# Strassen's seven parts for the inner quarter of two of FFN's products, not one

## The chip, the cores and the metric

The kernel runs on one core of one Trainium2 chip. The metric is the device time of one execution in microseconds: the median of three runs before the change is 1860.95 us (1859.37 to 1862.06).

## The reference, cut to what matters

Two layers, each with a half-step SwiGLU, a gated mixer and a second half-step SwiGLU, on 512 tokens of width 1024; the hidden width of SwiGLU is 2816. The change touches SwiGLU alone, which runs four times (the four FFNs).

```python
def swiglu(x, w_in, w_out):
    gu = x @ w_in
    g, u = jnp.split(gu, 2, axis=-1)
    return (jax.nn.silu(g) * u) @ w_out

for l in range(DEPTH):
    x = x + 0.5 * swiglu(rms_norm(x, ffn1_norm[l]), ffn1_w_in[l], ffn1_w_out[l])
    x = x + mixer(rms_norm(x, mix_norm[l]), ...)
    x = x + 0.5 * swiglu(rms_norm(x, ffn2_norm[l]), ffn2_w_in[l], ffn2_w_out[l])
```

## The kernel before, in words

**Precision.** Every operand of a product is split into a high part (fp32r, by ScalarE's copy) and a low part (operand less high part, by VectorE), and a product is three matmuls: high by high, high by low, low by high. For weights these are `Item.upper` and `Item.lower`: `whi` (L199, L201) and `wlo` (L206, L208).

**Weights.** They lie in DRAM as granules of 128 x 1024 (0.5 MB). `stage_items` writes the list of items in the order in which the products use them; `Stream` loads eight items ahead (`FETCH`) into nine buffers named `raw`, from SyncE's queue (L158). Where a granule is needed as a sum, a second transfer adds another granule to the loaded one, on GpSimd's queue (L160), or VectorE adds one buffer to another (`Item.sum`, L194). `whi` and `wlo` have three buffers each, so splitting runs at most some two granules ahead of TensorE.

**FFN's first product.** The 2816 columns of gate and up are 256 plain ones (`cl`) and five blocks of 512 each. A block's product (512 tokens by 1024, times 1024 by 512 gate and 512 up) is a two-by-two product of halves, which Strassen's scheme makes of seven products, numbered 1 to 7: the weights' quarters are a, b (gate) and c, d (up), and the operands of x are `acts[1]` to `acts[7]`. One product is two granules, 24 matmuls of 128x512 into two PSUM banks (`product`, L386 to L389). `snap` (L620) copies a bank to SBUF, `less` (L625) subtracts a copy from a bank, `gate` (L755) applies silu, and `times` (L761) multiplies gate by up. The result is transposed by TensorE into `at` tiles (`to_at`, L643, L647), the second product's operands.

**Pairs.** Blocks 1 and 2, and 3 and 4, form pairs. In both blocks of a pair product 2 multiplies the same lower-left quarter of x, by b of the first block and by b of the second. Side by side these make a two-by-two product again, which is done in seven inner parts of 6 matmuls each (`inner`, `inner_parts`, `inner_split`) instead of 2 x 24. Five inner parts stand in the first block and two in the second (`INNER`), and each is joined to the block's sums by a VectorE instruction of 128x512 (L833, L846, L847, L854, L857, L863, L870 in `pair_block`).

**FFN's second product.** `steps` lists its seven products in three chunks of columns (`o`, L386 to L389). Its operand 4 is a difference of two `at` tiles, made by VectorE (`comb`, L774), in the last FFN by ScalarE's negation and an adding transfer from SBUF to SBUF on GpSimd's queue (L1135, L1136).

**Order.** Each engine's instructions run in the order of its own queue. In the first block of the first FFN, and at the ends of the second products, the order is written out by hand; elsewhere a scheduler has set it. TensorE starts with nine matmuls on zeros (`WARM`, L146) while the first loads come.

Of the kernel before, what the change touches and what calls it, by code (L numbers as in the profile page):

```python
# [17 lines left out]
P = 128  # L18
# [11 lines left out]
WARM = 9  # L30
# [5 lines left out]
ORDER_P = (1, 5, 6, 7, 3, 4)  # L36
INNER = (((5, 1), (6, 5), (7, 2), (3, 6), (4, 3)), ((6, 7), (7, 4)))
# [61 lines left out]
def encoder_kernel(  # L99
# [120 lines left out]
    def stage_items():  # L220
        items, st = [], 0

        def add(*a, **k):
            items.append(Item(*a, stage=st, **k))
# [40 lines left out]
        def ffn(s):  # L265
            first = not items
            for g in range(4):
                add(Raw((s, "cl", g)), parts=2 if first and g < 2 else 1, pieces=2 if first and g == 0 else 1)
            for j in range(NB):
                if not j:  # L270
                    four(s, lambda q: q, j, (1024, 1024), ORDER_0 if first else ORDER_W)
                    continue
                if j in PAIRS:
                    key = [[(s, "b", j + z, g) for g in range(2)] for z in range(2)]
                    a, b, c = Raw(key[0][0]), Raw(key[0][1]), Raw(key[1][0], 1024, key[0][0])
                    d, d2 = Raw(key[1][1], 1024, key[1][0]), Raw(key[1][1])
                    parts = {1: (a, None, True), 2: (b,), 3: (d, b), 4: (d2,), 5: (d,), 6: (d, a), 7: (c,)}
                inner = dict(INNER[j not in PAIRS])
                for m in strassen(s, lambda q: q, j, (1024, 1024), ORDER_P):
                    if m in inner:  # L280
                        add(*parts[inner[m]])
                add(*parts[inner[0]]) if 0 in inner else None
# [344 lines left out]
    def stage_ffn(norm, nxt, late):  # L627
# [57 lines left out]
        def inner_parts(src):  # L685
# [7 lines left out]
            fine["t"] = t  # L693

        def inner_split():
            t = fine.pop("t")
            h = slot(F32R, "vh", (4, 2, P))
            l = scope_pool[0].tile([P, 4, 2, P], F32R, tag="vl", name=nm("vl"), bufs=1)
            split(h, l, t)
            fine.update({5: (h[:, 0], l[:, 0]), 6: (h[:, 1], l[:, 1]), 7: (h[:, 2], l[:, 2]), 4: (h[:, 3], l[:, 3])})  # L700
            for m, (i, b) in ((1, (0, 0)), (2, (1, 0)), (3, (1, 1))):
                fine[m] = [z[1][:, 2 * i : 2 * i + 2, b * P : (b + 1) * P] for z in (hx, lx)]
# [10 lines left out]
        with tc.manual_schedule(engines={mybir.EngineType.DVE, mybir.EngineType.Activation}) if first else nullcontext():  # L713
# [11 lines left out]
            inner_parts(b21)  # L725
# [95 lines left out]
        kept = {}  # L821

        def pair_block(jb, late_at):

            one = jb in PAIRS
# [4 lines left out]
            if one:  # L830
                qa = kept["a"] = bank("qA")
                inner(qa, 1, True)
                V.tensor_tensor(s1[:, 0, :], qa, s1[:, 0, :], ALU.add)  # L833
# [3 lines left out]
            qa = kept["a"]  # L837
            if one:
                qb = bank("qB")
                inner(qb, 5, True)  # L840
                tb = kept["s"] = slot(F32, "sq", (2, T))[:, 0, :]
                S.activation(tb, qb, AF.Copy)
            else:
                tb = kept["s"]
                inner(qa, 7, False)
                V.tensor_tensor(tb, qa, tb, ALU.subtract)  # L846
                V.tensor_tensor(s1[:, 1, :], tb, s1[:, 1, :], ALU.subtract)  # L847
# [3 lines left out]
            if one:  # L851
                qc = bank("qC")
                inner(qc, 2, True)
                V.tensor_tensor(s1[:, 0, :], qc, s1[:, 0, :], ALU.subtract)  # L854
            else:
                inner(qa, 4, False)
                V.tensor_tensor(s1[:, 0, :], qa, s1[:, 0, :], ALU.subtract)  # L857
                z1 = gate(s1, 0)
            product(pa, acts[7], K4, False, again=True)
            less(pa, sb)  # L860
            if one:
                inner(qa, 6, False)
                V.tensor_tensor(s1[:, 1, :], qa, s1[:, 1, :], ALU.add)  # L863
# [3 lines left out]
            times(z2, [sb[:, 0, :], sb[:, 1, :]], 1)  # L867
            if one:
                inner(qb, 3, False)
                V.tensor_tensor(s1[:, 1, :], qb, s1[:, 1, :], ALU.subtract)  # L870
                z1 = gate(s1, 0)
            if jb == NB - 1:
# [4 lines left out]
            late_at += [(z2, 1, 2 + 4 * jb, 4), (z1, 0, 2 + 4 * jb, 4)]  # L877
# [222 lines left out]
        for i, (m, c, _) in enumerate(steps):  # L1100
# [32 lines left out]
            if late and m == 6:  # L1133
# [1011 lines left out]
```

## Time and profile before

| what | value |
|---|---|
| median of three runs | 1860.95 us |
| profiled execution | 1859.66 us |
| its span on the core | 1857.9 us |
| TensorE, VectorE, ScalarE, GpSimd busy | 99%, 84%, 65%, 11% |
| matmuls and transposes | 9561 |
| read from HBM | 404.49 MB |

A row of a group names line, engine, operation, out<-in and count, then busy time, mean of one in ns, idle time before it, and what ended that. A row of a window names the stretch, its length, each engine's busy time with the number of instructions, the granted clock (1.00 is full), the share of the 16 transfer engines and GB/s. A busy PE is a union of overlapping matmuls: one shows 389 ns, while the next starts after some 227.

### The profile page before, as it was taken

The numbers are of one execution on the slowest core, as the hardware profiler recorded it, in microseconds if no ns is written. First come the engines' busy times: TensorE is split into PE (matmuls) and PEld (weight loads), VectorE is DVE, ScalarE is ACT, GpSimd is POOL, SyncE is SP. The second block draws the span as 40 slices with busy tenths as digits, with TensorE's granted clock in tenths as the row PEclk, the third lists the DMA queues.
The fourth block names the chain that finished last, engine by engine and source line by source line (L and its number), as shares of the span: only waits on it lengthen the run. The fifth ranks groups of instructions, "written<-read, shape, count | busy, mean of one in ns | idle before, by whom it ended". The sixth has DMA issues, their size and how long they took to land.

```text
span 1857.9 us, 26118 instructions
## 1 busy us (share of the span) xinstructions
PE 1847.8 (99%) x9561; PEld 1574.3 (85%) x9561; DVE 1556.5 (84%) x1915; ACT 1203.1 (65%) x1787; POOL 196.8 (11%) x235
## 2 busy tenths in 40 slices
PE   9999999999999999999999999999999999999998
PEld 7888888889998888888888888888899988888886
DVE  8888899758879787889978788996687797878999
ACT  6766666758656656666665666667676576656665
POOL 0010010100211011101001110110002100110010
PEclk9999999999999999999999999999999999999999
DMA  9788788875998479869757986987649985798695
GB/s 299 228 248 222 226 237 265 255 190 137 247 258 218 133 209 258 231 200 266 238 147 208 254 231 201 258 270 239 199 131 262 234 227 131 221 243 238 197 274 182
DMA packets 118384, 413.94 MB, mean 223 GB/s; under 512 B 13408, under 2 KB 13536, under 8 KB 118256
## 3 DMA queue, kind: packets, MB, share of 16 engines
q1 hardware_dynamic: 85712, 297.78, 45.7%
q0 software_dynamic: 32112, 113.71, 32.6%
q8 instruction: 75, 1.23, 0.3%
q10 hardware_dynamic: 432, 0.79, 0.1%
q14 instruction: 53, 0.43, 0.1%
HBM read 404.49 MB, written 6.29 MB: 221 GB/s over the span
## 4 chain that ended last, share of the span: by engine, by line
PE 97%; DMA 1%; DVE 1%; issue 0%; ACT 0%; POOL 0%; ACTq 0%; DVEq 0%; SPq 0%; POOLq 0%
PE A L386 9%; PE A L389 9%; PE A L387 9%; PE o L389 7%; PE o L386 7%; PE o L387 7%; PE B L386 5%; PE B L387 5%; PE B L389 5%; PE ps L386 3%; PE ps L387 3%; PE ps L389 3%; PE tr L643 2%; PE cl L387 2%; PE cl L389 2%; PE cl L386 2%
## 5 line engine op out<-in xcount | busy, mean ns | idle before, releaser
L208 DVE TENSOR_TENSOR wlo<-raw,whi 128x1024 fp32r<-128x1024 f32 (+1 forms) x540 | 638.7, 1191 | 170.3 <-ACT whi L201 169.3
L201 ACT ACTIVATE whi<-raw 128x1024 fp32r<-128x1024 f32 (+1 forms) x540 | 555.2, 1034 | 317.8 <-PE A L387 89.7
L160 POOL DMA_DIRECT2D raw<-in_wst_dram x186 | 161.4, 873 | 1458.9 <-DMA raw<-in_wst_dram 766.5
L194 DVE TENSOR_TENSOR raw<-raw,raw 128x1024 f32<-128x1024 f32 (+1 forms) x144 | 171.2, 1193 | 2.7
L387 PE MATMUL A<-whi,xl 128*128 128x512 f32 x320 | 124.5, 389 | 0.0
L386 PE MATMUL A<-whi,xh 128*128 128x512 f32 x320 | 124.5, 389 | 0.0
L199 ACT ACTIVATE whi<-raw 128x1024 fp32r<-128x1024 f32 x84 | 87.1, 1037 | 42.1 <-issue 21.5
L206 DVE SCALAR_TENSOR_TENSOR wlo<-raw,whi 128x1024 fp32r<-128x1024 f32 x84 | 99.8, 1196 | 4.6 <-ACT whi L199 4.5
L389 PE MATMUL A<-wlo,xh 128*128 128x512 f32 x320 | 92.1, 389 | 0.0
L620 ACT ACTIVATE sn<-A 128x512 f32<-128x512 f32 x96 | 56.2, 591 | 46.4 <-PE A L389 46.4
L755 ACT ACTIVATE th<-sn,r 128x512 f32<-128x512 f32 x80 | 56.1, 715 | 46.2 <-DVE sn L625 42.5
L389 PEld LDWEIGHTS A<-wlo,xh 128*128 128x128 f32 x320 | 60.1, 188 | 12.5
L387 PEld LDWEIGHTS A<-whi,xl 128*128 128x128 f32 x320 | 60.1, 188 | 12.5
L386 PEld LDWEIGHTS A<-whi,xh 128*128 128x128 f32 x320 | 60.1, 188 | 12.4
L386 PE MATMUL B<-whi,t1h 128*128 128x512 f32 x160 | 63.0, 394 | 0.0
L386 PE MATMUL A<-whi,t2h 128*128 128x512 f32 x160 | 62.5, 391 | 0.0
L387 PE MATMUL B<-whi,xl 128*128 128x512 f32 x160 | 62.3, 390 | 0.0
L387 PE MATMUL B<-whi,t1l 128*128 128x512 f32 x160 | 62.3, 389 | 0.0
L387 PE MATMUL A<-whi,t2l 128*128 128x512 f32 x160 | 62.3, 389 | 0.0
L386 PE MATMUL A<-whi,t3h 128*128 128x512 f32 x160 | 62.2, 389 | 0.0
L387 PE MATMUL A<-whi,t3l 128*128 128x512 f32 x160 | 62.2, 389 | 0.0
L386 PE MATMUL B<-whi,xh 128*128 128x512 f32 x160 | 62.2, 389 | 0.0
(498 smaller groups left out, 4909.2 us busy)
## 6 DMA issues: line engine op xcount, KB each, us to landing
raw<-in_wst_dram SPq DMA_DIRECT2D x503, 512.0 KB
raw<-in_wst_dram POOLq DMA_DIRECT2D x200, 512.0 KB, 8.2
raw<-in_wst_dram SPq DMA_DIRECT2D x28, 256.0 KB
vc<-vd SPq DMA_DIRECT2D x28, 256.0 KB
bm<-in_near_dram SPq DMA_DIRECT2D x16, 384.0 KB
vd<-v SPq DMA_DIRECT2D x8, 512.0 KB
dft<-in_dft_dram POOLq DMA_DIRECT2D x4, 514.0 KB, 8.3
x<-in_xin_dram SPq DMA_DIRECT2D x4, 512.0 KB
```

Source lines behind the costliest of these rows:

```text
L160: z = G.dma_start(out=self.t, in_=wst[GRAN_AT[plus]][:, 0 : self.n], accum_op=ALU.add)
L194: V.tensor_tensor(self.raw.t, self.raw.t, self.add.t, ALU.add)
L199: S.activation(self.out[0][:, cs], self.raw.t[:, cs], AF.Copy, scale=-1.0)
L201: S.activation(self.out[0][:, cs], self.raw.t[:, cs], AF.Copy)
L206: self.last = V.scalar_tensor_tensor(lo, t, -1.0, hi.bitcast(F32), ALU.mult, ALU.subtract)
L208: self.last = V.tensor_tensor(lo, t, hi.bitcast(F32), ALU.subtract)
L386: PE.matmul(ps, lh, rh, start=start, stop=False, skip_group_check=again)
L387: PE.matmul(ps, *((lh, rl) if w == "l" else (ll, rh)), start=False, stop=False, skip_group_check=again)
L389: PE.matmul(ps, *((ll, rh) if w == "l" else (lh, rl)), start=False, stop=stop, skip_group_check=again)
L620: S.activation(t[:, b, :], ps[b], AF.Copy)
L643: PE.transpose(tr[:, k, b * P : (b + 1) * P], a[:, b, (q + k) * P : (q + k + 1) * P], ident)
L755: S.activation(th[:, b, :], g[:, b, :], AF.Silu, scale=norm.r[:, c : c + 1])
```

## The change

1. In a pair, product 4 of both blocks multiplies the same quarter of x as well (`t4`, from `b21 - b22`), by d of the first block and by d of the second. Both products 4 are taken out, and seven more inner parts d1 to d7 come in, with operands of their own (`inner_parts("d", b21)`, two splits). `pair_block`, called for each block, becomes `pair_blocks`, called for each pair. Part d2 is accumulated into the bank of the first block's upper half, and d4 into that of the second block's, so that fewer joins are needed. The first block now has six inner parts, the second eight.
2. Operand 4 of the second product is made by ScalarE and an adding transfer in all four FFNs.
3. `WARM` is 12 instead of 9.

```diff
-WARM = 9
+WARM = 12
-ORDER_P = (1, 5, 6, 7, 3, 4)
-INNER = (((5, 1), (6, 5), (7, 2), (3, 6), (4, 3)), ((6, 7), (7, 4)))
+ORDER_P = (1, 5, 6, 7, 3)
+INNER = (
+    {1: "b1", 5: "b5", 6: "b2", 7: "b6 d2", 3: "b3"},
+    {1: "d1", 5: "d5 b7", 6: "d6 b4", 7: "d3", 3: "d7 d4"},
+)
...
                 if j in PAIRS:
+                    parts = {}
+                    for q in "bd":
+                        key = [[(s, q, j + z, g) for g in range(2)] for z in range(2)]
+                        a, b, c = Raw(key[0][0]), Raw(key[0][1]), Raw(key[1][0], 1024, key[0][0])
+                        d, d2, b2 = Raw(key[1][1], 1024, key[1][0]), Raw(key[1][1]), Raw(key[0][1])
+                        of = {1: (a, None, True), 2: (b,), 3: (d, b if q == "b" else b2), 4: (d2,), 5: (d,), 6: (d, a), 7: (c,)}
+                        parts.update({f"{q}{m}": z for m, z in of.items()})
...
-                (lambda c=c: part(0, 0, c)) if late
-                else (lambda c=c: comb(part(1, 0, c), part(1, 0, c), part(0, 0, c), ALU.subtract)),
+                lambda c=c: part(0, 0, c),
...
+        def pair_blocks(jb):
...
+            product(pa, acts[7], K4, False, again=True)
+            less(pa, sb)
+            inner(qa, "b6", False)
+            V.tensor_tensor(half(s1, 1), qa, half(s1, 1), plus)
+            inner(pa[0], "d2", False)
+            product(pb, acts[3], K4, False, again=True)
+            less(pb, s2)
+            ua = snap(pa)
...
+            inner(rb, "d5", True)
+            S.activation(tq, rb, AF.Copy)
+            inner(qa, "b7", False)
+            V.tensor_tensor(tb, qa, tb, sub)
+            V.tensor_tensor(half(s1, 1), tb, half(s1, 1), sub)
...
+            inner(rb, "d3", False)
+            V.tensor_tensor(half(ua, 1), rb, half(ua, 1), plus)
+            times(za, [half(ua, 0), half(ua, 1)], 0)
...
+            inner(ra, "d7", False)
+            V.tensor_tensor(tq, ra, tq, sub)
+            V.tensor_tensor(tq, pa[1], tq, plus)
...
+            inner(pa[0], "d4", False)
+            S.activation(tb, ra, AF.Copy)
+            V.tensor_tensor(tb, pa[0], tb, plus)
+            times(z1, [tb, tq], 0)
...
-            product(pa, acts[4], K4, False, again=True)
-            times(z1, pa, 0)
...
                 if jb == 1:
-                    inner_split()
-                pair_block(jb, late_at)
+                    inner_parts("d", b21)
+                    inner_split("b", [z[1][:, :, 0:256] for z in (hx, lx)])
+                    inner_split("d", t4)
...
-            if late and m == 6:
+            if m == 6:
                 t = part(0, 0, c)
                 S.activation(t, t, AF.Copy, scale=-1.0)
                 G.dma_start(out=t, in_=part(1, 0, c), accum_op=ALU.add)
```

On TensorE, in the second block of the third FFN's first pair, the first granule of product 4 stands behind product 3 (`A` is the pair of banks, `xh` and `xl` the quarter of x; another granule of 12 matmuls follows). Before:

```order
L386 MATMUL A_1752_9531<-whi_1797_9756,xh_1470_8061 128x512
L387 MATMUL A_1752_9531<-whi_1797_9756,xl_1471_8062 128x512
...
L386 MATMUL A_1753_9532<-whi_1797_9756,xh_1470_8061 128x512
L387 MATMUL A_1753_9532<-whi_1797_9756,xl_1471_8062 128x512
...
L389 MATMUL A_1752_9531<-wlo_1798_9757,xh_1470_8061 128x512 x2
L389 MATMUL A_1753_9532<-wlo_1798_9757,xh_1470_8061 128x512 x2
```

At the same place after the change stand d7 (bank `rA`) and d4 (bank `A`), with the split operands `vh` and `vl`:

```order
L394 MATMUL rA_1814_9704<-whi_1858_9922,vh_1737_9329 128x512
L395 MATMUL rA_1814_9704<-whi_1858_9922,vl_1738_9330 128x512
...
L397 MATMUL rA_1814_9704<-wlo_1859_9923,vh_1737_9329 128x512 x2
L394 MATMUL A_1803_9652<-whi_1860_9938,vh_1737_9329 128x512
L395 MATMUL A_1803_9652<-whi_1860_9938,vl_1738_9330 128x512
...
L397 MATMUL A_1803_9652<-wlo_1861_9939,vh_1737_9329 128x512 x2
```

Twenty-four matmuls became two times six here; the other five parts with a d stand between earlier products of the pair.

On VectorE, early in the third FFN's second pair: low parts of product 5's two granules, sums for product 6 (`raw` with `raw`), the join of the first inner part (`sn` with `qA`), and the sum for product 3 with the granule loaded last (`raw_1827` before, `raw_1894` after). Before:

```order
L208 TENSOR_TENSOR wlo_1814_9856<-raw_1790_9712,whi_1813_9855 128x1024
L194 TENSOR_TENSOR raw_1790_9712<-raw_1790_9712,raw_1779_9656 128x1024
L208 TENSOR_TENSOR wlo_1824_9904<-raw_1793_9732,whi_1823_9903 128x1024
L194 TENSOR_TENSOR raw_1793_9732<-raw_1793_9732,raw_1782_9674 128x1024
L833 TENSOR_TENSOR sn_1815_9871<-qA_1822_9902,sn_1815_9871 128x512
L208 TENSOR_TENSOR wlo_1829_9919<-raw_1796_9753,whi_1828_9918 128x1024
L194 TENSOR_TENSOR raw_1796_9753<-raw_1796_9753,raw_1786_9695 128x1024
L208 TENSOR_TENSOR wlo_1832_9938<-raw_1790_9712,whi_1831_9937 128x1024
L194 TENSOR_TENSOR raw_1790_9712<-raw_1790_9712,raw_1827_9916 128x1024
```

After:

```order
L211 TENSOR_TENSOR wlo_1878_10027<-raw_1851_9881,whi_1877_10026 128x1024
L211 TENSOR_TENSOR wlo_1888_10075<-raw_1854_9903,whi_1887_10074 128x1024
L197 TENSOR_TENSOR raw_1851_9881<-raw_1851_9881,raw_1841_9832 128x1024
L197 TENSOR_TENSOR raw_1854_9903<-raw_1854_9903,raw_1844_9845 128x1024
L844 TENSOR_TENSOR sn_1879_10042<-qA_1886_10073,sn_1879_10042 128x512
L211 TENSOR_TENSOR wlo_1893_10090<-raw_1857_9919,whi_1892_10089 128x1024
L197 TENSOR_TENSOR raw_1857_9919<-raw_1857_9919,raw_1848_9862 128x1024
L211 TENSOR_TENSOR wlo_1896_10109<-raw_1851_9881,whi_1895_10108 128x1024
L197 TENSOR_TENSOR raw_1851_9881<-raw_1851_9881,raw_1894_10106 128x1024
```

The two sums now stand together behind both low parts. On SyncE's queue the loads at this place were, before, `raw_1827` as the first behind the buffers freed by the sums:

```order
L158 DMA raw_1804_9811<-in_wst_dram 128x1024
L158 DMA raw_1809_9833<-in_wst_dram 128x1024
L158 DMA raw_1812_9852<-in_wst_dram 128x1024
L158 DMA raw_1827_9916<-in_wst_dram 128x1024
L158 DMA raw_1830_9935<-in_wst_dram 128x1024
```

After, `raw_1891` (the granule of d2) goes ahead of `raw_1894` and takes the buffer that the first of the two sums frees:

```order
L161 DMA raw_1873_10004<-in_wst_dram 128x1024
L161 DMA raw_1876_10023<-in_wst_dram 128x1024
L161 DMA raw_1891_10087<-in_wst_dram 128x1024
L161 DMA raw_1894_10106<-in_wst_dram 128x1024
L161 DMA raw_1899_10129<-in_wst_dram 128x1024
```

Over the whole program TensorE has 9516 matmuls and transposes instead of 9561 (48 fewer in the pairs, 3 warming ones more), VectorE 24 more low parts, 16 more sums of granules and 48 more joins and 9 fewer differences of `at` tiles, SyncE's queue 16 more loads, and GpSimd's queue 16 more adding transfers of granules and 9 more of `at` tiles.

More of the change, by code (lines that the diff above doesn't have):

```diff
@@ L819, in second @@
             less(pc, s1)
-        kept = {}
-        def pair_block(jb, late_at):
-            one = jb in PAIRS
+        sub, plus = ALU.subtract, ALU.add
+        def pair_blocks(jb):
+            f0 = 2 + 4 * jb
+            half = lambda t, b: t[:, b, :]
             pa = pair("A")
@@ L829, in pair_block @@
             settle_at()
[L830 to L833, printed above, removed]
+            qa = bank("qA")
+            inner(qa, "b1", True)
+            V.tensor_tensor(half(s1, 0), qa, half(s1, 0), plus)
             pb = pair("B")
@@ L836, in pair_block @@
             sb = snap(pb)
[L837 to L847, printed above, removed]
+            qb = bank("qB")
+            inner(qb, "b5", True)
+            tt = slot(F32, "sq", (2, T))
+            tb, tq = half(tt, 0), half(tt, 1)
+            S.activation(tb, qb, AF.Copy)
             settle_at()
@@ L860, in pair_block @@
             less(pa, sb)
[L861 to L863 removed]
+            inner(qa, "b6", False)
[4 more added lines that the diff above has]
+            ua = snap(pa)
+            z2 = gate(s2, 1)
+            times(z2, [half(sb, 0), half(sb, 1)], 1)
+            late_at.append((z2, 1, f0, 4))
```

80 lines of the change are left out of this document (49 added, 31 removed).

## The prediction

> **What bounds the kernel now.** I read the page first: how busy the engines are, the slices, and the chain of work that ended last.
>
> ```profile
> span 1857.9 us, 26118 instructions
> PE 1847.8 (99%) x9561; PEld 1574.3 (85%) x9561; DVE 1556.5 (84%) x1915; ACT 1203.1 (65%) x1787; POOL 196.8 (11%) x235
> ...
> DMA  9788788875998479869757986987649985798695
> ...
> PE 97%; DMA 1%; DVE 1%; issue 0%; ACT 0%; POOL 0%; ACTq 0%; DVEq 0%; SPq 0%; POOLq 0%
> ```
>
> TensorE works for 99% of the span and is 97% of the chain. The kernel can become shorter only by fewer products, and only while VectorE (84%) and the transfers (slices of 9) still deliver every granule in time. So the second view is the table by stage, for the third FFN: the two halves of its first pair of blocks, then a stretch of its second product, a piece of that stretch, and the second product of the last FFN. The columns are the stretch, its length, and busy time of PE, PEld, DVE, ACT and POOL (with instructions), then clock, DMA share and GB/s.
>
> ```profile
> 996.40:1037.61 41.21, 41.21 (x193) 34.36 (x191) 36.05 (x36) 25.74 (x33) 4.37 (x5) 1.00 0.79 226
> 1037.61:1074.73 37.12, 37.12 (x174) 30.98 (x173) 27.59 (x29) 22.17 (x29) 3.78 (x5) 1.00 0.87 238
> ...
> 1160.00:1240.00 80.00, 80.00 (x355) 66.24 (x354) 79.48 (x83) 48.02 (x58) 9.65 (x12) 1.00 0.93 273
> ...
> 1191.00:1201.00 10.00, 10.00 (x46) 8.29 (x45) 10.00 (x10) 5.82 (x7) 2.60 (x3) 1.00 1.04 329
> ...
> 1746.93:1846.00 99.07, 98.65 (x442) 80.98 (x440) 94.61 (x103) 63.38 (x79) 13.10 (x15) 1.00 0.82 229
> ```
>
> In the pair PE never idles: 78.33 of 78.33 us. In the second product it does not idle either, with VectorE at 99% and the transfers at 0.93 over 80 us and at 1.04 (full) over 10 us. Only the last FFN loses 0.42 us.
>
> **Products taken out.** The chain merges equal pieces and gives the pace.
>
> ```profile
> 996.40 1.75 PE tr L643 x16
> 1001.34 0.91 PE B L389 x4
> ```
>
> Four products take 0.91 us and sixteen transposes 1.75 us. A product over four granules' halves has 24 matmuls, an inner part has 6. Before, a pair has 12 x 24 + 7 x 6 = 330 matmuls and 32 transposes; 78.33 less 3.50 leaves 74.83 us, 0.2268 us each. After, it has 10 x 24 + 14 x 6 = 324. There are eight pairs (two in each of four FFNs), so 48 matmuls go: 48 x 0.2268 = **10.9 us** off the path, if every remaining matmul comes at the same pace.
>
> **What VectorE gets.** The groups of the same pair, kept apart by shape, give the durations (busy, then the mean in ns).
>
> ```profile
> L208 DVE TENSOR_TENSOR wlo<-raw,whi 128x1024 fp32r<-128x1024 f32 x26 | 31.7, 1223 | 11.6 <-ACT whi L201 11.6
> ...
> L194 DVE TENSOR_TENSOR raw<-raw,raw 128x1024 f32<-128x1024 f32 x10 | 12.3, 1225 | 0.3
> ...
> L206 DVE SCALAR_TENSOR_TENSOR wlo<-raw,whi 128x1024 fp32r<-128x1024 f32 x5 | 6.0, 1222 | 0.0
> ...
> L761 DVE SCALAR_TENSOR_TENSOR th<-sn,r,th 128x512 f32<-128x512 f32 x4 | 3.0, 745 | 0.0
> L625 DVE TENSOR_TENSOR sn<-B,sn 128x512 f32<-128x512 f32 x4 | 2.8, 692 | 1.3 <-PE B L389 1.3
> ...
> L870 DVE TENSOR_TENSOR sn<-qB,sn 128x512 f32<-128x512 f32 x1 | 0.7, 689 | 0.0
> ```
>
> Per pair come 3 low parts (3 x 1.22), 2 sums of raw granules (2 x 1.23) and 6 joins of 128x512 (6 x 0.69): 10.3 us. VectorE goes from 63.6 of 78.3 us to 73.9 of 77.0, or 96%. The halves are uneven. The first has 16 low parts, 6 sums, 4 `less`, 2 `times` and 4 joins, 33.9 us of durations. The second has 18, 6, 4, 6 and 9, 42.8 us. In the pair of before, durations add up to 66.5 us where 63.6 us are busy (neighbours overlap), a factor of 0.957: 32.5 us against 37.1 us of PE (156 matmuls and 16 transposes) in the first half, and 41.0 us against 39.9 us (168 and 16) in the second. So the second half is 1.1 us short, with 4.6 us to spare in the first. What covers this is VectorE's lead:
>
> ```profile
> 1042.36 1.22 DVE L208 TENSOR_TENSOR wlo<-raw,whi 128x1024 fp32r<-128x1024 f32 x1 [2.85 <-ACT whi L201]
> ...
> 1047.82 1.07 PE L389 MATMUL A<-wlo,t2h 128*128 128x512 f32 x4
> ```
>
> The low part is done at 1043.58 and read at 1047.82, 4.2 us later. It could not be earlier, since it waited 2.85 us for ScalarE, which waited for a free one of three buffers. A shortage of 1.1 us fits into a lead of 4.2 us and is made good in the next first half. I cost it at 0. Without this cover it would be 1.1 us a pair, 8.8 us in all.
>
> The four differences for the inner parts and their split are now made twice: 4 x 0.42 + 1.22 = 2.9 us of VectorE once per FFN, ahead of the first inner part, behind the same lead.
>
> ```profile
> L689 DVE TENSOR_TENSOR v<-xr 128x256 f32<-128x256 f32 x4 | 1.7, 419 | 0.0
> ...
> L394 DVE TENSOR_TENSOR vl<-v,vh 128x1024 fp32r<-128x1024 f32 x4 | 4.9, 1220 | 0.0
> ```
>
> ```profile
> L201 ACT ACTIVATE whi<-raw 128x1024 fp32r<-128x1024 f32 x27 | 28.6, 1060 | 16.9 <-PE A L387 8.5 <-issue 3.5 <-PE B L387 3.0
> ...
> L620 ACT ACTIVATE sn<-A 128x512 f32<-128x512 f32 x8 | 4.7, 591 | 4.8 <-PE A L389 4.8
> ```
>
> ScalarE gets 3 high parts, 2 snaps and 2 copies a pair, some 3 x 1.06 + 4 x 0.59 = 5.5 us on top of 47.9 of 78.3: it stays near 70%. New joins, snaps and gates wait for PE, and behind each in its queue stands the next granule's high or low part; in the rows of the order those parts are two to three granules ahead of PE, so I take 0 here too.
>
> **What the transfers get.** Queues in the same pair (packets, MB, share of all engines), and their issues:
>
> ```profile
> q1 hardware_dynamic: 3600, 13.11, 48.5%
> q0 software_dynamic: 1357, 4.97, 33.8%
> ...
> raw<-in_wst_dram SPq DMA_DIRECT2D x25, 512.0 KB
> raw<-in_wst_dram POOLq DMA_DIRECT2D x10, 512.0 KB, 8.5
> ```
>
> A load takes 0.485 x 78.33 / 25 = 1.52 us of all engines, an adding transfer 0.338 x 78.33 / 10 = 2.65 us. A pair now needs 27 and 12: 41.0 + 31.8 = 72.8 of 77.0 us, a share of 0.95 (before 0.83). The second product shows 1.04 for 10 us without an idle PE, so 0.95 is no limit by itself. But again the halves differ: 12 and 5, 31.5 of 37.1 us; 15 and 7, 41.4 of 39.9 us. The tightest spot is product 3's lower-left granule, loaded one buffer late, which a sum on VectorE wants soon after. Before:
>
> ```profile
> 996.45 0.33 SPq L158 DMA_DIRECT2D raw<-in_wst_dram  x1
> ...
> 1004.11 1.23 DVE L194 TENSOR_TENSOR raw<-raw,raw 128x1024 f32<-128x1024 f32 x1
> ...
> 1013.70 0.33 SPq L158 DMA_DIRECT2D raw<-in_wst_dram  x1
> ...
> 1017.70 0.87 POOL L160 DMA_DIRECT2D raw<-in_wst_dram  x1 [23.60 <-DMA raw<-in_wst_dram]
> ```
>
> The load had 7.7 us; a load in a quiet moment takes 4.0 us (issue at 1013.70, its adding transfer released at 1017.70). Now the first buffer that comes free goes to the new inner part, so between the sum that frees the second one and the sum that needs the load stand one join, two low parts and one sum: (0.69 + 3 x 1.22) x 0.957 = 4.2 us. VectorE's lead adds 4.2 less the 1.1 us that the second half before it was short, 3.1 (an estimate), so the load has 7.3 us before PE feels it. The bounds are 0 and what the slowest load in sight would cost (below); I take 0.5 us for all pairs, near the quiet load.
>
> **Part 4's differences.** For three FFNs, three VectorE differences go (2 x 1.22 + 0.96 us) and three ScalarE negations and three transfers on POOL's queue come. VectorE there is at 99% and PE does not wait for it, so nothing is gained. The last FFN has worked in the new way all along.
>
> ```profile
> L774 DVE TENSOR_TENSOR at<-at,at 128x1024 f32<-128x1024 f32 x30 | 36.6, 1221 | 0.0
> ...
> 1781.05 9.81 DMA raw<-in_wst_dram
> ...
> 1817.27 0.73 PE L389 MATMUL o<-wlo,c5h 128*128 128x512 f32 x2 [0.27 <-DVE wlo L208]
> ```
>
> It loses 0.42 us to a load that took 9.81 us and a late low part. On POOL's queue the next granules' adding transfers stand behind each new one. The lower end is 0, the upper end is 3 x 2.65 = 8 us an FFN if all their time came onto the path; I take the nearest row, 0.42 us x 3 = **+1.3 us**.
>
> **Twelve warming products.**
>
> ```profile
> 1.23 4.02 PE L146 MATMUL ps<-warm 128*128 128x512 bf16 x9 [1.23 <-DVE warm L143]
> 6.37 1.20 PE L379 MATMUL cl<-whi,xh 128*128 128x512 f32 x4 [1.12 <-ACT whi L201]
> ```
>
> Nine come every 0.43 us and end at 5.25; the first real product waits for ScalarE until 6.37 and goes at full pace at once (1.20 us for four with the tail). Twelve at 0.427 us are through at 1.23 + 12 x 0.427 = 6.35, just ahead of 6.37. So the three fill a gap: 0. The Trainium skill, "TensorE: Matmul & The Clock Gate", section "What's actually happening", says that the full clock is granted after about 3.4 us of work, counted in a window that runs freely, so the moment changes from run to run. The trace agrees that the pace had doubled by 6.37, and one trace cannot show the change from run to run; by the rule, a run with a later grant would save under 1.3 us (3 x 0.43, an estimate), and the sum would be that much lower in such a run.
>
> **Sum.** The profiled execution took 1859.66 us, 1.76 us around its span: 1859.66 - 10.9 + 0.5 + 1.3 = 1850.6. The median of the three runs is 1860.95, 1.3 us above it, which would give 1851.9. I forecast **1851.0 us**.
>
> **Rivals.** A measurement of this kernel can tell about 0.2% (3.7 us) from no change.
> 1. VectorE becomes the bound in second halves. For it: 41.0 us of work against 39.9. Against it: the 4.2 us lead, and 80 us at 99% without an idle PE. Price: 1.1 us x 8 pairs, about 8.8 us, so 1859.4.
> 2. Slower: the load for product 3's sum comes late in every first half. VectorE's queue stops at that sum, and the low parts of the next granules stand behind it. With a load of 9.81 us, as in the last FFN, it comes 9.81 - 7.3 = 2.5 us too late for PE, 20 us in eight pairs: 1850.6 + 20 = 1871. It decides above 7.3 us, and the net gain of 9.1 us, 1.1 a pair, is gone at 8.4 us. For it: 41.4 us of transfers in the 39.9 us of the second half before. Against it: that half's last adding transfers end before this load, and quiet loads take 4 us.
> 3. Part 4's transfers collide with the second product's full stretch more than in the last FFN, and loads in the pairs are late now and then: 1 to 2 us each in three FFNs and a few pairs, 1855.5.
> That the matmuls are not saved is excluded: the built order has 9516 matmuls against 9561 (48 fewer, 3 warming ones more).
>
> **How the numbers follow.** Forecast, 1848 to 1853.5: 0.67. Below 1848: 0.03 (without the two charges the sum is 1848.8, and the runs spread by 2.7 us). Rival 3, 1853.5 to 1857.2: 0.14. Rival 1, 1857.2 to 1864.7: 0.09. Rival 2, above 1864.7: 0.07. Faster by over 0.2% (below 1857.2): 0.84; within: 0.09; slower: 0.07. The range 1847.5 to 1857.5 leaves out about 0.18.
>
> **What would show it.** Each pair should last about 77.0 us with PE busy throughout; otherwise a step failed. If rival 1 holds, matmuls that read wlo wait for VectorE near products 7, 3 and the two last inner parts of second halves. If rival 2 holds, VectorE's sums of raw granules show idle time released by DMA in first halves. If rival 3 holds, PE idles in the second products of the first three FFNs behind raw transfers. The gap ahead of 6.37 us should be gone, and DMA's share in pairs should be near 0.95. The prediction is wrong if pairs show idle PE of more than a microsecond each.

## The result, and the profile after

The changed kernel takes 1870.07 us (median of four runs, 1868.77 to 1872.15), beside 1860.17 of the kernel before in the same rounds: a ratio of 1.0053, with a 95% interval of 1.0041 to 1.0066. It is slower by 9.9 us; the forecast was 9 to 10 us faster. The profiled execution took 1871.23 us.

The page of the kernel after:

```profile
span 1869.5 us, 26281 instructions
...
PE 1844.7 (99%) x9516; PEld 1563.0 (84%) x9516; DVE 1619.9 (87%) x2014; ACT 1249.3 (67%) x1856; POOL 218.2 (12%) x260
...
PE 85%; DMA 7%; DVE 6%; issue 2%; ACT 1%; ACTq 0%; DVEq 0%; SPq 0%
```

The matmuls did go (9516 instead of 9561, although three warming ones came in), and TensorE is busy for less time. But the chain that ended last, 97% TensorE before, now runs for 7% over DMA and 6% over VectorE. The waits of TensorE (waiting matmul and line, what released it, total, times, longest; c1h is the high part of the second product's first operand, th a gated result that TensorE transposes):

```profile
PE o L394 <- ACT c1h L401: 4.2, 4, 1.1
PE tr L651 <- DVE th L773: 4.0, 4, 1.6
PE A L397 <- DVE wlo L211: 2.8, 4, 1.5
...
PE o L397 <- DVE wlo L211: 1.2, 1, 1.2
```

Where they lie shows the table by stage of the third FFN: the halves of the first pair, then those of the second.

```profile
999.35:1036.48 37.13, 37.13 (x174) 30.98 (x173) 32.90 (x34) 25.63 (x34) 3.46 (x4) 1.00 0.75 219
1036.48:1076.34 39.86, 39.86 (x185) 33.19 (x184) 36.91 (x42) 26.63 (x34) 6.05 (x7) 1.00 0.96 276
1076.34:1114.49 38.15, 37.74 (x173) 30.82 (x172) 34.31 (x35) 25.43 (x35) 4.32 (x5) 1.00 0.87 239
1114.49:1153.36 38.87, 35.41 (x161) 28.32 (x159) 32.76 (x36) 23.31 (x31) 2.59 (x3) 1.00 0.89 258
```

The first pair lasts 76.99 us, as forecast (77.0), with TensorE always busy, though its second half has the transfers at 0.96 and VectorE at 93%. The second pair loses 3.9 us of TensorE's time: 0.4 in its first half, 3.5 in its second. How one of these comes about stands in the chain of the second FFN's second pair, read in order of time (start, length, what):

```profile
805.58 9.05 DMA raw<-in_wst_dram
...
814.73 1.07 ACT whi L204
...
816.97 0.75 DVE th L773
817.71 1.14 DVE wlo L211
818.85 1.20 DVE sn L633 x2
```

The transfer is the adding transfer for d7's granule. The granule's load was issued by SyncE at 801.32, the adding transfer followed at 805.58, and ScalarE's high part started at 814.73, as soon as the sum had landed. VectorE had nothing else that its queue would let it do. On TensorE, VectorE and ScalarE that reads:

```profile
817.77 0.98 PE L651 MATMUL tr<-ident,th 128*128 128x128 f32 x7 [1.07 <-DVE th L773]
...
822.57 0.73 PE L394 MATMUL o<-whi,c1h 128*128 128x512 f32 x2 [1.09 <-ACT c1h L401]
```

```profile
815.82 1.23 DVE L211 TENSOR_TENSOR wlo<-raw,whi 128x1024 fp32r<-128x1024 f32 x1 [2.46 <-ACT whi L204]
```

```profile
814.73 2.01 ACT L204 ACTIVATE whi<-raw 128x1024 fp32r<-128x1024 f32 x2 [4.25 <-DMA raw<-in_wst_dram]
...
819.49 1.34 ACT L767 ACTIVATE th<-sn,r 128x512 f32<-128x512 f32 x2 [1.80 <-DVE sn L633]
...
821.68 0.84 ACT L401 ACTIVATE c1h<-at 128x768 fp32r<-128x768 f32 x1
```

ScalarE idles 4.25 us for the landing and VectorE 2.46 for ScalarE. Behind d7's low part in VectorE's queue stand `th` (which the transposes ahead of d7 need) and `less` (`sn`); behind `less`, on ScalarE, the gate, and behind the gate the second product's first operand, c1h. So one late granule shows as two waits of TensorE, neither of which names it, and neither is for d7. ScalarE idles for this granule in all eight pairs, between 2.8 and 4.3 us each; in the four first pairs TensorE feels next to nothing of it in that half (one stop of 0.2 us).

The third wait has the place of the forecast's second rival. In the third FFN (the chain, then VectorE, then TensorE):

```profile
1083.11 5.13 DMA raw<-in_wst_dram
1088.54 0.95 issue
1089.48 1.23 DVE wlo L211
```

```profile
1088.34 1.23 DVE L197 TENSOR_TENSOR raw<-raw,raw 128x1024 f32<-128x1024 f32 x1 [1.16 <-DMA raw<-in_wst_dram]
```

```profile
1090.76 0.73 PE L397 MATMUL A<-wlo,t2h 128*128 128x512 f32 x2 [0.34 <-DVE wlo L211]
```

The load for product 3's sum is issued at 1083.11, when the buffer comes free, and the sum wants it before it has landed. Of the 1.16 us that the sum waits TensorE feels 0.34.

The table gives the medians, and beside them sums over the four FFNs, from the first matmuls' starts in each kernel's one profile: "first" is from block 0 to the end of the first product, "second" the second product. The forecast for "first" was 782.9 - 10.9 = 772.0, and 0.5 for the pairs' transfers. All but the first two rows are explained with their experiments below.

| kernel | median us | ratio to before, 95% | first | second |
|---|---|---|---|---|
| before | 1860.2 | 1 | 782.9 | 433.3 |
| after | 1870.1 | 1.0041 to 1.0066 | 789.2 | 437.5 |
| make early | 1868.3 | 1.0030 to 1.0057 | 782.1 | 444.2 |
| no settle | 1872.0 | 1.0051 to 1.0076 | 786.9 | 442.9 |
| d2 behind 3 | 1862.5 | 1.0006 to 1.0024 | 780.2 | 438.0 |
| all three | 1872.1 | 1.0053 to 1.0078 | 783.8 | 447.0 |
| part 4 and warming alone | 1861.1 | 0.9997 to 1.0015 | 782.9 | 434.4 |
| three moves | 1862.9 | 1.0007 to 1.0024 | 775.2 | 441.2 |
| short joins | 1880.4 | 1.0098 to 1.0129 | 793.7 | 441.4 |
| moves, plain loads | 1854.4 | 0.9963 to 0.9983 | 772.2 | 437.0 |
| moves, d7 grown | 1853.5 | 0.9951 to 0.9976 | 772.2 | 436.9 |
| moves, b7 and d7 grown | 1853.3 | 0.9947 to 0.9974 | 772.2 | 436.5 |
| after, plain loads | 1855.0 | 0.9960 to 0.9982 | 773.0 | 435.2 |
| after, d7 grown | 1854.8 | 0.9961 to 0.9979 | 775.4 | 435.4 |
| after, d7 plain | 1855.3 | 0.9963 to 0.9988 | 773.6 | 436.9 |
| after, d5 plain | 1863.7 | 1.0011 to 1.0028 | 783.0 | 435.8 |
| d7 grown, part 4 undone | 1856.7 | 0.9975 to 0.9993 | 772.2 | 440.1 |

### The profile page after: what moved, and what is told of

It reads as the page before. It is cut to its first block, busy times and chain, and to the rows that moved or that the text cites. A ratio compares the mean times of both kernels' runs of the same rounds, so it can differ in the third digit from the quotient of the medians.

```text
span 1869.5 us, 26281 instructions
## 1 busy us (share of the span) xinstructions
PE 1844.7 (99%) x9516; PEld 1563.0 (84%) x9516; DVE 1619.9 (87%) x2014; ACT 1249.3 (67%) x1856; POOL 218.2 (12%) x260
## 4 chain that ended last, share of the span: by engine, by line
PE 85%; DMA 7%; DVE 6%; issue 2%; ACT 1%; ACTq 0%; DVEq 0%; SPq 0%
PE A L394 7%; PE A L395 7%; PE A L397 7%; PE o L395 7%; PE o L397 7%; PE o L394 6%; DMA raw<-in_wst_dram 6%; PE B L394 4%; PE B L397 4%; PE B L395 4%; PE ps L394 3%; PE ps L395 3%; PE ps L397 3%; DVE wlo L211 2%; PE cl L395 2%
## 5 line engine op out<-in xcount | busy, mean ns | idle before, releaser
L204 ACT ACTIVATE whi<-raw 128x1024 fp32r<-128x1024 f32 (+1 forms) x556 | 569.4, 1034 | 299.9 <-PE A L395 79.9
L211 DVE TENSOR_TENSOR wlo<-raw,whi 128x1024 fp32r<-128x1024 f32 (+1 forms) x556 | 657.1, 1192 | 126.0 <-ACT whi L204 123.6
L163 POOL DMA_DIRECT2D raw<-in_wst_dram x202 | 175.0, 879 | 1441.3 <-DMA raw<-in_wst_dram 697.5
L197 DVE TENSOR_TENSOR raw<-raw,raw 128x1024 f32<-128x1024 f32 (+1 forms) x160 | 190.6, 1196 | 8.7 <-DMA raw<-in_wst_dram 7.1
L394 PE MATMUL A<-whi,xh 128*128 128x512 f32 x208 | 80.9, 389 | 0.0
L395 PE MATMUL A<-whi,xl 128*128 128x512 f32 x208 | 80.9, 389 | 0.0
L397 PE MATMUL A<-wlo,xh 128*128 128x512 f32 x208 | 60.2, 389 | 0.0
L792 DVE SCALAR_TENSOR_TENSOR x<-o,x 128x512 f32<-128x512 f32 x80 | 52.0, 687 | 0.6 <-PE o L397 0.4
L394 PE MATMUL ps<-xh,whi 128*128 128x512 f32 x128 | 50.7, 396 | 0.0
L651 PE MATMUL tr<-ident,th 128*128 128x128 f32 x352 | 46.5, 274 | 4.0 <-DVE th L773 4.0
```

The source lines that it names most:

```text
L163: z = G.dma_start(out=self.t, in_=wst[GRAN_AT[plus]][:, 0 : self.n], accum_op=ALU.add)
L197: V.tensor_tensor(self.raw.t, self.raw.t, self.add.t, ALU.add)
L204: S.activation(self.out[0][:, cs], self.raw.t[:, cs], AF.Copy)
L211: self.last = V.tensor_tensor(lo, t, hi.bitcast(F32), ALU.subtract)
L394: PE.matmul(ps, lh, rh, start=start, stop=False, skip_group_check=again)
L395: PE.matmul(ps, *((lh, rl) if w == "l" else (ll, rh)), start=False, stop=False, skip_group_check=again)
```

## The experiments

**Moves in the queues.** The first theory took the three waits for three places: c1h behind the gate, transposes ahead of d7, d2's load ahead of product 3's.

*Operand 1 made earlier:*

```diff
             late_at.append((za, 0, f0, 4))
+            if jb + 2 == NB:
+                make(0)
+                make(1)
             product(pb, acts[3], K4, False, again=True)
...
-            if jb + 2 == NB:
-                make(0)
-                make(1)
             inner(pa[0], "d4", False)
```

> Theory (three separate places in the queues of ScalarE and VectorE, not the amount of transfers or of VectorE's work): operand 1 of the second product, made one product earlier, takes away the four waits of PE for c1h (4.2 us and some 0.27 us of slow restart each): 1870.1 - 5.3 = 1865, between 1864 and 1867. The waits for th and for wlo stay. Rival A (transfers bound the pairs: the share is near full and every granule lands just in time): the same granules land at the same time, the wait moves to d7 or d4, 1869 to 1871. Rival B (VectorE is full in the second half): 2.2 us of its work put earlier delays the low parts of d7 and product 3, 1870 or more.

Measured: 1868.3. The waits for c1h are gone, but the time is not:

```profile
PE o L397 <- DVE wlo L211: 3.0, 4, 1.2
PE A L397 <- DVE wlo L211: 2.6, 4, 1.2
PE o L397 <- DVE wlo L209: 2.0, 3, 0.7
PE rA L397 <- DVE wlo L211: 1.8, 3, 1.0
```

New waits for low parts stand in the second product and at d7 (bank `rA`). The first products gave up 7.1 us and the second ones took 6.7.

*No transposes ahead of d7* (`settle_at()` there is dropped; the tile waits for the next one):

```diff
-            settle_at()
             inner(ra, "d7", False)
```

> Theory: without the transposes ahead of d7 the waits of PE for th go (4.0 us), but PE comes to the second product earlier and waits longer for c1h, which gains only ScalarE's two copies out of the way, 0.95 us a place: 1870.1 - 3.8 = 1866.3, between 1865 and 1868, with the waits for c1h grown to 6 us or more. Rival A (transfers): d7's granule lands as late as before and PE waits for it instead, 1869 to 1871. Rival B (VectorE full): 1869 to 1871.

Measured: 1872.0. As expected the waits for th go and those for c1h grow, but the edit makes a wait of its own: four more transposes stand ahead of the next pair's first inner part (`qA`), which waits for ScalarE to copy them out.

```profile
PE qA L394 <- ACT at L655: 6.2, 4, 2.0
PE o L394 <- ACT c1h L401: 5.3, 4, 1.4
```

It settles nothing between the theories.

*d2 behind product 3*, so that the loads for product 3's sum come one buffer earlier:

```diff
-    {1: "b1", 5: "b5", 6: "b2", 7: "b6 d2", 3: "b3"},
+    {1: "b1", 5: "b5", 6: "b2", 7: "b6", 3: "d2 b3"},
...
-            inner(pa[0], "d2", False)
             product(pb, acts[3], K4, False, again=True)
             less(pb, s2)
+            inner(pa[0], "d2", False)
             ua = snap(pa)
```

> Theory: with the inner part d2 behind product 3, the loads for product 3's sum come one buffer earlier, as in the kernel before; the waits for wlo of product 3 (2.8 us in four first halves, and the restarts) go: 1870.1 - 3.6 = 1866.5, between 1865.5 and 1868. Rival A (transfers): as many bytes in the same time, so d2's or b3's granule is late instead, 1869 to 1871; and a new wait for bank A, whose snapshot comes 1.4 us later, could cost up to 1 us in each of eight pairs, 1872 to 1878.

Measured: 1862.5, 7.6 us less, twice what was expected and outside the range. No matmul of the first products waits for wlo any more, and the waits for th are halved (2.0). The order in a queue matters, then; but the first products are still 8 us above the forecast.

*The three together:*

> All three edits at once. Theory: PE passes from d4 to the second product without a wait, d7's low part is ready 0.3 us late at most, product 3's sum is in time: (c1h and th together some 3.1 us in three FFNs and 1.4 in the first, 10.5) and 3.6 us: 1870.1 - 14 = 1856, between 1853 and 1859, the rest above 1850.6 being in the second products. Rival A (transfers bound the pairs): the first products stay 15 us or more above the forecast, 1866 to 1871. Rival B (VectorE full): pairs of 1.1 us each above, 1860 to 1864.

Measured: 1872.1, above the theory's numbers and rival A's too, with both side effects above present (5.9 us for qA, 5.3 in the second product for wlo). The theory of three separate places falls; these side effects keep the run from deciding between the rivals.

**Part 4 and the warming products alone**, in the kernel before:

```diff
-WARM = 9
+WARM = 12
...
-                (lambda c=c: part(0, 0, c)) if late
-                else (lambda c=c: comb(part(1, 0, c), part(1, 0, c), part(0, 0, c), ALU.subtract)),
+                lambda c=c: part(0, 0, c),
...
-            if late and m == 6:
+            if m == 6:
```

> The kernel before with the change's two other parts alone: part 4's differences by ScalarE and transfers in the first three FFNs, and twelve warming products; the first products are those of before. Theory (the loss is in the pairs and in the lead with which VectorE leaves them; these two parts are as good as free): 1860.1 + 0 to 1.3 - 0.2, so 1859.5 to 1861.5. Rival (part 4's transfers collide in the full stretch of the second products, which carries the 2.5 us that the first three second products grew by): 1862 to 1864.

Measured: 1861.1, not told from no change. In its profile one second product of four is longer, by 1.1 us. The loss is not here.

**Three moves that take nothing from VectorE:** d2 behind product 3 as above, the transposes between d7 and d4, and c1h alone ahead of `less`.

```diff
             product(pb, acts[3], K4, False, again=True)
+            low0 = upper_half() if jb + 2 == NB else None
             less(pb, s2)
...
-            settle_at()
             inner(ra, "d7", False)
             V.tensor_tensor(tq, ra, tq, sub)
+            settle_at()
             V.tensor_tensor(tq, pa[1], tq, plus)
             if jb + 2 == NB:
-                make(0)
+                low0()
                 make(1)
```

> The changed kernel with d2 behind product 3 (1862.5), and two moves that cost VectorE nothing: the transposes stand behind d7 instead of ahead of it, and c1h alone (not its low part) is made ahead of the gate. Theory of places in the queues: the waits for c1h (3.6 us in four) and for th (2.0 in four), with 0.27 us of restart each, go: 1862.5 - 7.8 = 1854.7, between 1853 and 1858. Rival (VectorE leaves the pair with no lead, and its queue is as long as before): the wait moves to the low parts that the second product's first matmuls read, and the time stays at 1861 to 1864.

Measured: 1862.9, the rival's number. The runs spread by 7.5 us (1859.4 to 1866.9; the kernel before by 2.6), and stops appear now here, now there. So far the order had been moved; the next two take load away instead.

*Nine joins of each second half on 32 of 512 columns:*

```diff
-            V.tensor_tensor(half(ua, 0), half(ua, 0), ra, sub)
+            V.tensor_tensor(half(ua, 0)[:, 0:32], half(ua, 0)[:, 0:32], ra[:, 0:32], sub)
```

> As the kernel with the three moves, but the nine joins of each pair's second half work on 32 of their 512 columns (the rest of the sums is left out, so this computes other numbers); all queues, waits and transfers stay. It takes some 9 x 0.6 = 5.4 us of VectorE's 41 us from each second half. If VectorE's fullness there (41.0 us of work in 39.9, and no lead left for the second product) is the cause, the pairs and the second products lose all their extra stalls: 1849 to 1853. If the transfers are the cause, granules land as late as before and the time is that of the three moves within 1.5 us.

Measured: 1880.4. It was meant as a test of VectorE's fullness and is not one: with cheaper joins the scheduler wrote another order. In the kernel with the moves the sum at 126.34 stands behind three low parts, two joins and another sum that follow the low part of 119.17, and waits for nothing; here it stands right behind that low part. Its load is issued 0.3 us earlier in this kernel (117.24 and 117.57). VectorE's sum, then TensorE:

```profile
125.55 1.23 DVE L197 TENSOR_TENSOR raw<-raw,raw 128x1024 f32<-128x1024 f32 x1 [5.03 <-DMA raw<-in_wst_dram]
```

```profile
127.96 1.22 PE L397 MATMUL A<-wlo,t2h 128*128 128x512 f32 x2 [3.00 <-DVE wlo L211]
```

VectorE has less to do and waits 5.03 us for one load. What the kernel shows is the price of a granule that is wanted too early.

*Plain loads for d5, d6 and d7* (no adding transfer), on the kernel with the moves:

```diff
+                        if q == "d":
+                            c, d = Raw(key[1][0]), Raw(key[1][1])
```

> As the kernel with the three moves, but the granules of d5, d6 and d7 are plain loads without their adding transfers (two a pair; the sums are left out, so this computes other numbers): the transfers of a pair go back to 10 adding ones, 67.5 of 77.0 us, a share of 0.88. VectorE's work stays. If the transfers are the cause, the stalls in the pairs go: 1849 to 1854. If VectorE's fullness is the cause, the time is that of the three moves within 1.5 us.

Measured: 1854.4, and the first products at 772.2, the forecast's length. VectorE has all its work in the same order. So what the pairs lose comes neither from the amount of VectorE's work nor from its order, but from these granules' transfers.

**d7's granule, with everything computed.** Of the granules of d, let K00 be the first one of the pair's first block and K10 the first one of its second block. d7 needs K10 + K00, and K00 is the addend of d6's sum, already in a buffer. Here the adding transfer adds K10 to it there, once the sum has read it, in place of a new load with an adding transfer behind it.

```diff
+                if self.grow:
+                    G.dma_start(out=self.add.t, in_=wst[GRAN_AT[self.grow]][:, 0 : self.raw.n], accum_op=ALU.add)
                 self.add = None
...
+                        if q in "d":
+                            of[6], of[7] = (d, a, key[1][0]), (a,)
```

> As the kernel with the three moves (1862.9), and d7's granule is no longer loaded with an adding transfer of its own: when the sum for d6 has read its addend, an adding transfer makes d7's granule of it in place. One load (1.52 us of all engines) fewer a pair, and the granule starts on its way some 9 us earlier; everything is still computed. Theory (transfers late in the pairs and their second halves are what is lost): 1857 to 1861, the waits near d7 and c1l gone. Rival (the shortage is VectorE's, or the waits come from the order alone): 1861.5 to 1864. Rival (the addend's buffer, now kept to d7, delays the loads for product 3's sum): above 1864.

Measured: 1853.5, faster than both kernels and better than expected.

> As the one before, for b7 too: two loads fewer a pair, but b1's granule then holds its buffer from b1 to b7, some 50 us, in place of two shorter stays. Theory of transfers: 1855 to 1860 if the engines' time counts, above the former if the number of free buffers counts: then the loads for product 3's sums come later, and the waits for wlo in the first halves return, 1864 to 1870.

Measured: 1853.3, the same. One load fewer a pair is worth nothing, and the buffer held longer costs nothing.

*The changed kernel with plain loads, nothing moved:*

> The changed kernel itself, no instruction moved, with plain loads for the granules of d5, d6 and d7 (their adding transfers are left out, so this computes other numbers). If late transfers alone make the loss, and the places in the queues matter only because the granules are late: 1853 to 1857, the waits for th and wlo gone and those for c1h below 1 us in all. If the places matter by themselves, the waits for c1h (4.2 us and restarts) and some of product 3's stay: 1858 to 1863. If VectorE's fullness makes the loss: 1866 to 1870.

Measured: 1855.0. VectorE's and ScalarE's instructions stand in the same order as in the changed kernel, and the waits for c1h, th and wlo are gone from the first products. With the granules in time the places cost next to nothing.

**Which granule.** Four more runs.

> The changed kernel with one edit: d7's granule grows by an adding transfer in the buffer of d6's addend, no instruction else moved, everything still computed. Theory (the granule of d7 is the root: load and adding transfer one after the other take as long as its buffer comes free ahead of use, and VectorE's queue stands behind it): 1854 to 1857, as without the adding transfers (1855.0). If the three moves are what made the version with them fast: 1860 to 1865.

Measured: 1854.8 with this one edit; VectorE's and ScalarE's instructions stand in the same order as in the changed kernel. All waits of 0.3 us or more in its profile, past the start:

```profile
PE A L408 <- DVE wlo L214: 1.7, 1, 1.7
...
PE o L408 <- DVE wlo L214: 1.2, 1, 1.2
...
PE o L405 <- ACT whi L207: 0.4, 1, 0.4
```

The one of 1.7 us is left over at the place of the second rival. In the second FFN's second pair the load of product 3's granule was issued at 748.30 and landed only just before 756.92, and here the sum waited 4.55 us for it (VectorE, then TensorE):

```profile
756.92 1.23 DVE L198 TENSOR_TENSOR raw<-raw,raw 128x1024 f32<-128x1024 f32 x1 [4.55 <-DMA raw<-in_wst_dram]
```

```profile
759.34 0.73 PE L408 MATMUL A<-wlo,t2h 128*128 128x512 f32 x2 [1.75 <-DVE wlo L214]
```

In the kernel with the three moves besides, no such stop is left (first products 772.2 against 775.4).

The table for the third FFN's pairs:

```profile
994.09:1031.22 37.13, 37.13 (x174) 30.98 (x173) 32.90 (x34) 25.63 (x34) 3.46 (x4) 1.00 0.77 219
1031.22:1071.08 39.86, 39.86 (x185) 33.19 (x184) 38.26 (x43) 26.71 (x34) 6.04 (x7) 1.00 1.00 273
1071.08:1108.21 37.13, 37.13 (x173) 30.98 (x172) 33.32 (x34) 25.88 (x36) 4.32 (x5) 1.00 0.89 241
1108.21:1142.80 34.59, 34.58 (x161) 28.54 (x159) 32.82 (x36) 23.47 (x31) 2.60 (x3) 1.00 0.93 271
```

The second half of the first pair has VectorE at 96% and the transfers at 1.00, fuller than in the changed kernel (93% and 0.96), and TensorE does not stop. Neither share is the bound. In the second FFN's second pair, the place of the chain above, the adding transfer for d7 is now issued 16.7 us before ScalarE takes the granule, at 808.21, with no wait for DMA (GpSimd's queue, then ScalarE's):

```profile
791.56 0.86 POOL L200 DMA_DIRECT2D raw<-in_wst_dram  x1 [2.02 <-ACT whi L207]
```

```profile
808.21 1.06 ACT L207 ACTIVATE whi<-raw 128x1024 fp32r<-128x1024 f32 x1 [0.30 <-PE rB L406]
```

That wait of 0.3 us, for TensorE, is the same in all eight pairs; ScalarE no longer idles for d7's granule.

> The changed kernel with a plain load for d7's granule alone (its adding transfer is left out, so this computes other numbers); d5's and d6's keeps its own. Theory of d7 as the root: 1855 to 1858. If the sum of the adding transfers' time counts, whichever they are: half of the way, 1861 to 1864. If d5's and d6's granule is the root: 1867 to 1871.

Measured: 1855.3; without d7's one adding transfer a pair nearly all of the loss is gone. The sum for product 3 in the third FFN waits here as long as in the changed kernel (1.40 us and 1.16), yet no matmul of the first products waits for wlo:

```profile
1080.16 1.22 DVE L197 TENSOR_TENSOR raw<-raw,raw 128x1024 f32<-128x1024 f32 x1 [1.40 <-DMA raw<-in_wst_dram]
```

> The changed kernel with a plain load for the granule of d5 and d6 alone (its adding transfer is left out, so this computes other numbers); d7's keeps its own. Theory of d7 as the root: 1866 to 1871. If the sum of the adding transfers' time counts: 1861 to 1864. If this granule is the root: 1855 to 1858.

Measured: 1863.7, a miss for d7 as the only root and inside the numbers of the second theory: 6.4 us less, with c1h's waits at 3.3 us and th's at 2.7. But both edits take one adding transfer a pair away, and one is worth 14.8 us and the other 6.4; together they take away 15.1. So it isn't the sum of the engines' time that counts. ScalarE still idles 2.2 to 4.1 us for d7's granule in every pair here, little less than in the changed kernel. How the neighbouring granule's transfer comes to cost 6.4 us is not shown.

> The kernel with the three moves and d7's granule grown in place (1853.5), with part 4's differences by VectorE again in the first three FFNs, everything computed. If part 4's transfers cost what the kernel before with parts 4 and the warming products alone showed (1.1 us at most): 1852 to 1853.5. If VectorE's 3.4 us an FFN that they save are needed in the second product, now that pairs leave it less lead: 1855 to 1860.

Measured: 1856.7, some 3 us more than with part 4 in the new way (1853.5; the two were run at different times, and their intervals to before just touch). The second products of the first and third FFN, of the kernel with d7 grown and the moves, then of this one:

```profile
222.09:331.99 109.90, 109.75 (x495) 89.66 (x494) 105.08 (x116) 74.90 (x98) 14.87 (x18) 1.00 0.85 245
1141.41:1250.10 108.69, 108.67 (x496) 89.93 (x494) 105.06 (x116) 75.05 (x98) 15.79 (x19) 1.00 0.86 255
```

```profile
222.10:332.68 110.58, 109.99 (x495) 89.59 (x494) 107.96 (x119) 72.63 (x95) 12.25 (x15) 1.00 0.79 231
1142.83:1253.22 110.39, 109.75 (x495) 89.59 (x494) 107.87 (x119) 72.61 (x95) 13.17 (x16) 1.00 0.81 238
```

VectorE's 2.8 us more each show as 0.7 and 1.7 us of length. Here VectorE's fullness does tell: the pairs now leave it with less lead.

## Why the prediction was wrong, step by step

- **Products taken out: right.** With d7's granule in time and the three moves the first products of the second to fourth FFN last 192.97 us where 195.65 stood: 2.68 us less each, forecast 2.72.
- **VectorE at 0: right in the pairs.** For a second half 41.0 us were reckoned; 38.3 are busy in the table with d7 grown alone, 96% of it, without a stop. It is the 43 instructions that were counted, but they overlap more than the factor of 0.957 allowed for, and some reach over the edges of the half. The first rival falls there. The second products stay 2 to 4 us (in all four) above before even in the fast kernels; that this is VectorE's lost lead is shown only as far as the last run goes (its own second products are 6.8 us above).
- **Transfers: the step that failed.** The prediction said: "so 0.95 is no limit by itself", which held, and "The tightest spot is product 3's lower-left granule [...] I take 0.5 us for all pairs". It looked for the place by the engines' time and by the granule that comes one buffer late, and overlooked that d7's granule is two transfers in a row: issue at 801.32, adding transfer from 805.58 to 814.63, 13.3 us in all, and ScalarE stood idle for the last 4.2 of them. The term measured about 15 us (1870.1 against 1854.8 with that granule alone made in another way). The 3.8 us by which that kernel still lies above the forecast are, in its profile, 2.9 in the first products (775.4 against 772.5, most of it around the one stop of 1.75 us) and 0.8 in the second (435.4 against 434.6 with part 4's charge).
- **"behind each in its queue stands the next granule's high or low part [...] so I take 0 here too": failed with it.** The queues did pass a lateness of some 2.5 us on to three other places. With the granule in time 0 is right.
- **The second rival** had the right sign and one of the places. That its time, 1871, is nearly the measured one is luck: the waits at its place are 2.8 us in all where it put 20, and d7's granule isn't in it. The 4.2 us from the load's issue to the sum were right (1083.11 to 1088.34, less 1.16 of waiting: 4.1), and the load took 5.13 where 4.0 was expected. What was missing is VectorE's lead, 3.1 us by the forecast. In the changed kernel 0.8 is left of it: of the sum's 1.16 us TensorE felt 0.34, and in the last FFN 1.49 of 2.33. With d7's granule in time and the same order it is 2.8: of 4.55 us TensorE felt 1.75, and of the last FFN's 2.65 us nothing. So the wait for d7's granule in the half before had used the lead up. And the rival's own case, a load too late even with the full lead, did come, once in eight pairs of that kernel.
- **Part 4: +1.3 forecast, 1.4 measured on the kernel before**, which cannot be told from 0. With the new pairs ahead of it the new way saves some 3 us, all of it in the second products (436.9 against 440.1).
- **Warming: 0 held, its working did not.** The page shows twelve warming products ending at 5.55 and the first real one waiting for ScalarE still:

```profile
1.23 4.32 PE L149 MATMUL ps<-warm 128*128 128x512 bf16 x12 [1.23 <-DVE warm L146]
6.20 0.50 PE L387 MATMUL cl<-whi,xh 128*128 128x512 f32 x1 [0.66 <-ACT whi L204]
```

The last three start 0.22 us apart, the earlier ones 0.43: they already run at full pace, so the gap shrinks from 1.12 to 0.66 us and does not close.

## What to carry to other kernels

Ask of every granule not only what its transfers cost in engine time but how long its way is, from the buffer that must come free over each transfer in a row to the use, and compare that with the time from release to use; shares of 1.00 were harmless here and 13 us of way were not. A late granule is found at the ends of queues that have nothing to do with it, so follow the chain of the waits to a DMA before moving instructions: five kernels with moves gained 7.6 us at most, the one granule 15.2. Where a sum of two buffers has read its addend, that buffer can grow into the next operand, without a load and far ahead of its use.

## What the runs showed of the hardware

In the chains above an adding transfer of 512 KB took 9.05 us from its issue, and a plain load 5.13. And a long stop can cost twice: in the kernel with the short joins TensorE stops for 3.00 us, and the stretch behind it runs at half the clock (last but two column).

```profile
124.00:128.00 4.00, 1.00 (x6) 0.50 (x4) 2.45 (x4) 0.25 (x1) 0.00 (x0) 0.92 0.50 172
128.00:134.00 6.00, 6.00 (x14) 4.74 (x15) 5.79 (x7) 3.21 (x5) 0.87 (x1) 0.50 0.54 178
```

Fourteen matmuls come in 6 us there, where 26 come at full pace, some 2.7 us lost on top of the stop. The length of the stop alone does not decide it. In the same kernel stretches at half the clock follow the stops of 2.71, 2.09 and 2.17 us as well, but none follows the one of 2.78 us that ends at 729.02. In the kernel without transposes ahead of d7 one follows a stop of 1.89 us, and none one of 1.98 us:

```profile
752.30:756.00 3.70, 3.70 (x16) 3.08 (x17) 3.32 (x5) 3.60 (x9) 0.00 (x0) 1.00 1.06 215
1083.00:1086.00 3.00, 3.00 (x9) 2.35 (x8) 2.62 (x4) 2.65 (x6) 0.00 (x0) 0.50 1.07 214
```

The stops of the changed kernel, up to 1.6 us, show no such rows.
